# Hybrid attention block on one core: the next block's logits are taken before the second map is added, the stick-breaking scan zeroes masked weights itself, and input sums and accumulating transfers get places in the engine orders

## The chip, the cores and the metric

The kernel runs on one core of a Trainium2 chip. The core has five engines with an instruction queue each: TensorE (PE, matrix products), VectorE (DVE, elementwise work and scans), ScalarE (ACT, lookups and copies), GpSimd (POOL, elementwise work and the DMAs that accumulate) and SyncE (SP, the other DMAs). Each queue is worked off in order; semaphores order the engines against each other. The metric is the device time of one execution in microseconds, lower is better.

## The reference, cut to what matters

512 tokens of width 1024 get 16 meta tokens in front (528 positions), a layer norm, and one large input projection. Its columns feed two attention branches: eight differential heads (two softmax maps each, the second subtracted with a learned factor `lam`) and sixteen stick-breaking heads. Both are causal. Gates, two branch projections, a merge, an output projection and a last layer norm follow.

```python
def diff_attn_block(q, k, v, q_pos, slopes, lam):
    ...
    s = jnp.where(dist >= 0, s + alibi[None, :, None], -jnp.inf)
    p = jax.nn.softmax(s, axis=-1)
    a = p[:, :, 0] - lam * p[:, :, 1]
    return jnp.einsum('bhqk,bhkd->bhqd', a.astype(v.dtype), v)

def stick_breaking_block(q, k, v, q_pos):
    k_pos = jnp.arange(k.shape[2])
    before = k_pos[None, :] < q_pos[:, None]
    z = jnp.einsum('bhqd,bhkd->bhqk', q, k).astype(jnp.float32) * (SB_HEAD_DIM ** -0.5)
    log_keep = jnp.where(before, jax.nn.log_sigmoid(-z), 0.0)
    suffix = lax.cumsum(log_keep, axis=3, reverse=True) - log_keep
    a = jnp.where(before, jnp.exp(jax.nn.log_sigmoid(z) + suffix), 0.0)
    return jnp.einsum('bhqk,bhkd->bhqd', a.astype(v.dtype), v)
```

## The kernel before

All tensors are float32. A product is made from a high part rounded to the PE's short float32 (`wh`, `hTh`) and a remainder (`wl`, `hTl`), in three matmuls: high by high, high by low, low by high. The weights come from HBM in halves of 128 x 512. For each half SP loads `raw` (L134), ACT casts it to `wh` (`hi`, L160) and DVE subtracts to get `wl` (`lo`, L165). `prep` does this four halves ahead of the half that PE multiplies, and then calls `fetch`, which issues loads as far as the ring buffers have room.

From the fourth unit on, keys and values of a unit are made together from seven products instead of eight (a Strassen-like scheme, `stage_kv`, matmuls at L626). It needs sums of the input, `tS` and `tl`, made once by `input_sums` (four calls; each has one small copy on POOL at L597, four DVE sums at L599 to L602, a cast on ACT at L604 and a subtraction on DVE at L605). It also needs sums of weight halves. For two of them, SP loads one half into a buffer `rawk` (L134) and a DMA issued by POOL adds the other half from HBM to it (L136, `accum_op`); DVE adds further ones (`add`, L147). The branch projections at the end do the same with `rawa`.

The middle of the program is a list of 16 units: eight differential heads (`d`), then eight pairs of stick-breaking heads (`s`). While PE makes the projections of the next units, `run` inserts the steps of the current unit at written times. For a `d` unit these are `d_scores`: for each of the four blocks of 128 queries (longest first: 528, 400, 272, 144 keys) and each of the two maps, PE makes logits (L692), DVE adds the bias and takes the row minimum (L775), ACT takes the exponential with its sum (L779). Then DVE takes reciprocals (L783), POOL scales the first map (L784) and multiplies the second factor by `nlam` (L785), and DVE adds the scaled second map into `apad` (L786). `transposed` turns `apad` on PE (L698, L703), ACT and DVE split it (`ah` L708, `al` L709), `d_values` multiplies by the values, and `d_norm` (with a Ln at L821 and an Exp at L823 on ACT) finishes the head one unit later. For an `s` unit, `s_scores` has ACT take two sigmoids per logit tile (L840, L842), POOL zero the weights on and right of the diagonal (L846), DVE run a product scan from the right (L848, against a mask `after` that holds the product at 1 over masked columns) and multiply (L849).

The order of the instructions on each engine is decided by the framework's scheduler, which lists instructions by a simulated timeline while it respects data dependencies. Two places are fixed by hand: `keep_order` holds the program order for the start and the tail, and `behind` chains chosen ACT instructions. `follow` adds such an order-only dependency between two instructions. In the middle part all else may be moved by the scheduler, also far ahead of where it was written.

Of the kernel before, what the change touches and what calls it, by code (L numbers as in the profile page):

```python
# [44 lines left out]
def hybrid_block_kernel(ctx: ExitStack, tc: tile.TileContext, x, meta, emb_g, emb_b, w_in, b_gate,  # L45
# [70 lines left out]
    raws, split, sums, later = {}, [], {}, []  # L116
# [8 lines left out]
    def fetch(most=99):  # L125

        while state["l"] < len(loads) and most:
            l = state["l"]
            src, more, tag = loads[l]
            bufs, log = rings[tag]  # L130
            if len(log) >= bufs and left[log[-bufs]] or tag not in pools:
                return
            raw = pools[tag].tile([P, 4, P], F32, tag=tag, name=tag, bufs=bufs)
            nc.sync.dma_start(raw if l < WOUT else raw.rearrange("p a b -> p (a b)"), src)  # L134
            if more is not None:
                g.dma_start(raw, more, accum_op=ALU.add)  # L136
            raws[l] = raw
            log.append(l)
            state["l"] += 1
            most -= 1  # L140

    def add(h):

        first, second = items[h]
        one = sums.pop(True) if first is None else raws[first]
        raw = one if first is None else pools["sum"].tile([P, 4, P], F32, tag="sum", name="sum", bufs=1)
        v.tensor_tensor(raw, one, raws[second], op=ALU.add)  # L147
        for l in items[h]:
            if l is not None:
                left[l] -= 1  # L150
        sums[h] = sums[True] = raw

    def hi(h):

        assert len(split) == h
        item = items[h]
        raw = raw0[:, h // 2, ts(h % 2, 4)] if item is None else sums.pop(h) if isinstance(item, tuple) else raws[item]
        wh, wl = [wpool.tile([P, 4, P], F32R, tag=w, name=w, bufs=6) for w in ("wh", "wl")]
        split.append((raw, wh, wl))
        s.copy(wh, raw)  # L160
# [30 lines left out]
    def behind(name, on=True):  # L191

        if on:
            ins = nc.cur_bb.bb.instructions[-1]
            if name in state:
                follow(ins, state[name])
            state[name] = ins

    def keep_order(first, engines=ORDERED):

# [318 lines left out]
    with tc.tile_pool(name="att", bufs=1) as ap:  # L519
# [17 lines left out]
        after, staged = [], []  # L537


        K = [ap.tile([P, 2, L], F32R, name=f"k{c}") for c in range(2)]  # L540
# [209 lines left out]
        def d_scores(unit, h):  # L750

            A = unit["A"]


            bias = ap.tile([P, L], F32, tag="bias", name="bias", bufs=2)
            if h == 0:
                g.iota(bias, pattern=[[-1, L]], base=400, channel_multiplier=1, allow_small_or_imprecise_dtypes=True)
                g.affine_select(bias, bias, pattern=[[-1, L]], compare_op=ALU.is_ge, fill=1e30, base=400,
                                channel_multiplier=1)
            g.tensor_scalar(bias, biases[-1] if h else bias, 0.5 if h else -0.5, None, op0=ALU.mult)  # L760
            biases.append(bias)
            a = apads[h % 2]
            mn = ap.tile([P, NB, 2, 2], F32, tag="mn", name="mn", bufs=2)
            zs = ap.tile([P, NB, 2], F32, tag="zs", name="zs", bufs=2)
            rz = ap.tile([P, NB, 2], F32, tag="rz", name="rz", bufs=2)
            for i in reversed(range(NB)):
                nk = NKEY[i]
                e = [E[c][:, ZOFF[i]:ZOFF[i] + nk] for c in range(2)]
                for c in range(2):
                    m = mn[:, i, c, :]  # L770
                    for n, (ps, k0, use) in enumerate(logits(A[c], K[c], i)):
                        if n == 1:
                            yield
                        b0 = 384 - P * i + k0
                        v.tensor_tensor_reduce(e[c][:, k0:k0 + use], ps[:, :use], bias[:, b0:b0 + use], -1.0, 3e38,  # L775
                                               ALU.add, ALU.min, m[:, n:n + 1])
                    if nk > 512:
                        v.tensor_tensor(m[:, 0:1], m[:, 0:1], m[:, 1:2], op=ALU.min)
                    s.activation(e[c], e[c], AF.Exp, scale=-1.0, bias=m[:, 0:1], accum_out=zs[:, i, c:c + 1])  # L779
                    if c == 0:  # L780
                        yield
                r = rz[:, i, :]
                v.reciprocal(r, zs[:, i, :])  # L783
                g.tensor_scalar(e[0], e[0], r[:, 0:1], None, op0=ALU.mult)  # L784
                g.tensor_tensor(r[:, 1:2], r[:, 1:2], nlam, op=ALU.mult)  # L785
                v.scalar_tensor_tensor(a[:, AOFF[i]:AOFF[i] + nk], e[1], r[:, 1:2], e[0], op0=ALU.mult, op1=ALU.add)  # L786
                yield

        def d_values(unit, ta):
            (vh, vl), vf = unit["V"]  # L790
# [39 lines left out]
        def s_scores(unit, c, first):  # L830
# [3 lines left out]
            for i in reversed(range(NB)):  # L834
# [7 lines left out]
                    s.activation(sg[:, o], ps[:, :use], AF.Sigmoid)  # L842
                    behind("act", first)

                own = sg[:, ds(z0 + nk - P, P)]
                g.affine_select(own, own, pattern=[[-1, P]], compare_op=ALU.is_gt, fill=0.0, base=0, channel_multiplier=1)  # L846
                rev = om[:, z0:z0 + nk][:, ::-1]
                v.tensor_tensor_scan(rev, rev, after[0][:, L - nk:][:, ::-1], 1.0, ALU.mult, ALU.max)  # L848
                v.tensor_tensor(a[:, ds(AOFF[i], nk - 1)], sg[:, ds(z0, nk - 1)], om[:, ds(z0 + 1, nk - 1)],  # L849
                                op=ALU.mult)  # L850
                yield
# [22 lines left out]
        def spread(gen, t0, dt, count):  # L874
            return [(t0 + dt * m, lambda: next(gen)) for m in range(count)]
# [12 lines left out]
        for u, (kind, n) in enumerate(UNITS):  # L888
# [9 lines left out]
            if u + 4 in (SEVEN + 1, SEVEN + 2):  # L898
                if not tS:
                    tS.append(ypool.tile([P, KT, L], F32R, tag="ys", name="tS"))  # L900
                for m in range(2):
                    steps.append((5.0 + 6.0 * m, lambda k=2 * (u + 3 - SEVEN) + m: input_sums(k)))
            if kind == "d":
                ta = {}
                steps += spread(d_scores(unit, n), 0.0, TD[0], 10)
                parts = transposed(ta, apads[n % 2], "d")
                steps += [(TD[1] + 0.7 * m, f) for m, f in enumerate(parts)]
                steps.append((TD[2], lambda: d_values(unit, ta)))
                pending = [(3.0 if n < 7 else 5.8, lambda unit=unit, n=n: d_norm(unit, n))]
# [268 lines left out]
```

## Time and profile before

| | value |
|---|---|
| time, median of 3 runs | 742.61 us (742.55 to 744.74) |
| the profiled execution | 746.39 us, of which the profile's span is 744.7 us |
| mean granted TensorE clock | 0.983 |
| PE busy | 716.7 us, 4546 matmuls |
| DVE busy | 597.4 us |
| ACT busy | 441.2 us |
| POOL busy | 212.3 us |
| HBM read and written | 82.53 MB and 7.86 MB |

The profile is of one execution. Times in its timeline are in microseconds from the start of the span. A row of the timeline gives start, duration, engine, line, operation, what is written and read, and in brackets the idle time of the engine just before it with the instruction that ended it. A row of the table by stretches gives, for each stretch of time, its length and the busy time of PE, of the PE's weight loads, of DVE, ACT and POOL with the number of instructions, the granted clock, and the DMA share and rate. PE, POOL and DVE overlap; the program ends when PE's products and the tail after them are done. SPq and POOLq mean the queue of an engine that issues DMAs.

### The profile page before, as it was taken

What the parts mean: (1) busy time and instruction counts of PE and PEld (TensorE: products, weight loads), DVE (VectorE), ACT (ScalarE), POOL (GpSimd) and SP (SyncE); (2) the same over time, 40 slices, a digit from 0 to 9 for tenths busy, and PEclk for the clock granted to TensorE, in tenths of its full rate; (3) what the DMA queues carried; (4) which work ended last, traced back from release to release, by engine and by line L of the source; (5) the groups of instructions that cost most, each with busy time, mean ns of one, the idle gap of its engine ahead of it and who ended that gap; (6) DMA issues with size and microseconds to landing.
All of it is one profiled execution on the core that took longest, in us unless ns stands there. A gap on an engine that the chain in (4) does not pass through costs nothing.

```text
span 744.7 us, 13453 instructions
## 1 busy us (share of the span) xinstructions
PE 716.7 (96%) x4546; PEld 651.2 (87%) x4546; DVE 597.4 (80%) x1214; ACT 441.2 (59%) x1043; POOL 212.3 (29%) x269
## 2 busy tenths in 40 slices
PE   8899999998999898999999999999999999999995
PEld 8799999987988787888989898988888998899885
DVE  6986678887888767979797989878566778688897
ACT  5675667676667966656656565656544555656300
POOL 3343453453463313232323121214002201240002
PEclk9989999999999998999999999999999999999998
DMA  9374444647555544455655524395229747787802
GB/s 291 89 153 119 133 98 114 162 104 164 141 113 130 136 128 108 135 123 144 140 158 117 140 90 126 104 304 147 71 83 184 157 100 180 147 169 186 320 27 105
DMA packets 160135, 105.02 MB, mean 141 GB/s; under 512 B 7441, under 2 KB 148146, under 8 KB 160066
## 3 DMA queue, kind: packets, MB, share of 16 engines
q1 hardware_dynamic: 137762, 91.04, 41.5%
q0 software_dynamic: 21984, 12.06, 12.8%
q10 hardware_dynamic: 320, 1.06, 0.4%
q8 instruction: 36, 0.59, 0.3%
q14 instruction: 33, 0.27, 0.1%
HBM read 82.53 MB, written 7.86 MB: 121 GB/s over the span
## 4 chain that ended last, share of the span: by engine, by line
PE 80%; DVE 7%; DMA 4%; POOL 3%; issue 3%; ACT 3%; SPq 0%; ACTq 0%; DVEq 0%; POOLq 0%
PE q L626 15%; PE ps L460 11%; PE ps L459 11%; PE ps L461 11%; PE q L985 9%; PE ps L475 6%; PE sc L692 5%; PE t L698 3%; DMA lgb<-in_ln_b_dram 1%; PE t L703 1%; DMA rawk<-in_w_in_dram 1%; PE bank L350 1%; PE av L862 1%; PE av L863 1%; POOL e L784 1%
## 5 line engine op out<-in xcount | busy, mean ns | idle before, releaser
L165 DVE TENSOR_TENSOR wl<-raw,wh 128x512 fp32r<-128x512 f32 x168 | 121.2, 726 | 41.7 <-ACT wh L160 40.2
L460 PE MATMUL ps<-hTl,wh 128*128 128x512 f32 x368 | 146.7, 399 | 0.0
L459 PE MATMUL ps<-hTh,wh 128*128 128x512 f32 x368 | 145.8, 396 | 0.0
L461 PE MATMUL ps<-hTh,wl 128*128 128x512 f32 x368 | 145.3, 395 | 0.0
L160 ACT CAST wh<-raw 128x512 fp32r<-128x512 f32 x168 | 102.9, 621 | 35.5 <-PE ps L460 20.6
L461 PEld LDWEIGHTS ps<-hTh,wl 128*128 128x128 f32 x368 | 69.6, 189 | 12.9
L459 PEld LDWEIGHTS ps<-hTh,wh 128*128 128x128 f32 x368 | 69.6, 189 | 12.8
L460 PEld LDWEIGHTS ps<-hTl,wh 128*128 128x128 f32 x368 | 69.6, 189 | 12.1
L692 PE MATMUL sc<-k,A 128*128 128x264 f32 (+3 forms) x320 | 66.7, 301 | 4.1 <-ACT e L842 2.3
L846 POOL TENSOR_SCALAR_AFFINE_SELECT e<-e 128x128 f32<-128x128 f32 x64 | 43.6, 702 | 93.0 <-ACT e L842 84.5
L985 PE MATMUL q<-gh,wl 128*128 128x256 f32 x224 | 63.9, 285 | 0.0
L985 PE MATMUL q<-gl,wh 128*128 128x256 f32 x224 | 63.7, 284 | 0.0
L985 PE MATMUL q<-gh,wh 128*128 128x256 f32 x224 | 63.2, 282 | 0.2 <-ACT t L994 0.2
L784 POOL TENSOR_SCALAR e<-e,rz 128x528 f32<-128x528 f32 (+3 forms) x32 | 46.1, 1441 | 56.9 <-DVE rz L783 56.9
L136 POOL DMA_DIRECT2D rawk<-in_w_in_dram x24 | 32.4, 1381 | 99.5 <-DMA rawk<-in_w_in_dram 62.2
L709 DVE TENSOR_TENSOR al<-t,ah 128x512 fp32r<-128x512 f32 (+2 forms) x88 | 45.7, 525 | 18.4 <-ACT ah L708 11.2
L692 PEld LDWEIGHTS sc<-k,A 128*128 128x128 f32 x320 | 51.4, 192 | 9.2 <-ACT e L842 2.7
L848 DVE TENSOR_TENSOR_SCAN e<-e,after 128x528 f32<-128x528 f32 (+1 forms) x64 | 55.4, 871 | 4.8 <-ACT e L840 4.6
L708 ACT CAST ah<-t 128x512 fp32r<-128x512 f32 (+2 forms) x88 | 40.1, 464 | 30.0 <-PE t L698 21.9
L626 PE MATMUL q<-tS,wh 128*128 128x264 f32 x192 | 56.0, 292 | 0.8 <-DVE A L552 0.7
L626 PE MATMUL q<-tl,wh 128*128 128x264 f32 x192 | 55.4, 289 | 0.0
L626 PE MATMUL q<-tS,wl 128*128 128x264 f32 x192 | 55.0, 288 | 0.0
(278 smaller groups left out, 1976.7 us busy)
## 6 DMA issues: line engine op xcount, KB each, us to landing
raw<-in_w_in_dram SPq DMA_DIRECT2D x140, 256.0 KB, 3.1
k<-ks SPq DMA_DIRECT2D x60, 132.0 KB, 2.7
rawk<-in_w_in_dram SPq DMA_DIRECT2D x24, 256.0 KB, 3.4
rawk<-in_w_in_dram POOLq DMA_DIRECT2D x24, 256.0 KB, 5.2
raw<-in_w_out_dram SPq DMA_DIRECT2D x16, 256.0 KB, 3.7
k<-ks SPq DMA_DIRECT2D x60, 66.0 KB, 2.2
raw<-in_w_br_diff_dram SPq DMA_DIRECT2D x12, 256.0 KB, 3.4
raw<-in_w_br_sb_dram SPq DMA_DIRECT2D x12, 256.0 KB, 4.2
```

What stands on the lines that cost most here:

```text
L160: s.copy(wh, raw)
L165: eng.tensor_tensor(wl, raw, wh.bitcast(F32), op=ALU.subtract)
L459: pe.matmul(ps, wh[:, k % 4, :], hTh[:, k, M:], start=(k == 0), stop=False)
L460: pe.matmul(ps, wh[:, k % 4, :], hTl[:, k, M:], start=False, stop=False)
L461: pe.matmul(ps, wl[:, k % 4, :], hTh[:, k, M:], start=False, stop=(k == KT - 1))
L475: pe.matmul(ps[:, :H2], a[:, k % 4, :], b[:, k, ts(c, H2)], start=(k == 0 and m == 0), stop=(k == KT - 1 and m == 2))
L626: pe.matmul(bank, a[:, k, :], b, start=start and k == 0 and j == 0, stop=k == 3 and j == 2, skip_group_check=not start)
L692: pe.matmul(ps[:, :n], q, K[:, m, k0:k0 + n], start=(m == 0), stop=(m == 1))
L709: v.tensor_tensor(l, t[:, o:o + w], h.bitcast(F32), op=ALU.subtract)
L784: g.tensor_scalar(e[0], e[0], r[:, 0:1], None, op0=ALU.mult)
L848: v.tensor_tensor_scan(rev, rev, after[0][:, L - nk:][:, ::-1], 1.0, ALU.mult, ALU.max)
L985: pe.matmul(bank, a[:, k, :], b[:, n, k, :], start=start and k == 0 and m == 0, stop=k == 3 and m == 2, skip_group_check=not start)
```

## The change

Four edits are made.

1. In `d_scores` the last step of a block (DVE adds the second map, formerly L786) is put off: it is kept in a list `last` and issued in the next block, once the first map's logits of that block have been taken. The last block's one gets an extra step, so `d_scores` has 11 steps instead of 10. On POOL the small product with `nlam` comes before the scaling of the first map.
2. In `s_scores` the zeroing of masked weights on POOL (L846) is removed. The scan starts at 0 and takes the larger of the product and a matrix `diag` that is 1 on the diagonal only, so that it is 0 right of the diagonal, 1 on it and the product left of it. `diag` is a zeroed tile with a copy of the identity.
3. `input_sums` is wrapped in `placed`, which makes the first instruction that it issues on each of PE, DVE, ACT and POOL follow the instruction written before it on that engine. The scheduler can't move it ahead of that place.
4. The accumulating transfers are no longer issued in `fetch`. They wait in `second` and are issued by `added`, two calls of `prep` later for `rawk` (or earlier, if `hi` or `add` wants the sum), and are `placed` on POOL. For `rawa` they are issued at once, as before, and placed.

```diff
             if more is not None:
-                g.dma_start(raw, more, accum_op=ALU.add)
+                second[l] = lambda raw=raw, more=more: g.dma_start(raw, more, accum_op=ALU.add)
+                later.append((state["n"] + (2 if tag == "rawk" else 0), lambda l=l: added(l)))
+                later.sort(key=lambda x: x[0])
+                if tag == "rawa":
+                    added(l)
...
+    def added(l):
+
+        if l in second:
+            placed(second.pop(l), ORDERED[3:])
+
     def add(h):
 
-        first, second = items[h]
+        first, other = items[h]
+        for l in items[h]:
+            added(l)
...
         item = items[h]
+        added(item)
...
+    def placed(work, engines=ORDERED):
+
+        ins = nc.cur_bb.bb.instructions
+        n = len(ins)
+        work()
+        for e in engines:
+            new = next((i for i in ins[n:] if i.engine == e), None)
+            old = next((ins[m] for m in range(n - 1, max(n - 400, 0), -1) if ins[m].engine == e), None)
+            if new is not None and old is not None:
+                follow(new, old)
...
+            last = []
             for i in reversed(range(NB)):
...
                     if c == 0:
                         yield
+                        if last:
+                            placed(last.pop(), ORDERED[1:2])
                 r = rz[:, i, :]
                 v.reciprocal(r, zs[:, i, :])
+                g.tensor_tensor(r[:, 1:2], r[:, 1:2], nlam, op=ALU.mult)
                 g.tensor_scalar(e[0], e[0], r[:, 0:1], None, op0=ALU.mult)
-                g.tensor_tensor(r[:, 1:2], r[:, 1:2], nlam, op=ALU.mult)
-                v.scalar_tensor_tensor(a[:, AOFF[i]:AOFF[i] + nk], e[1], r[:, 1:2], e[0], op0=ALU.mult, op1=ALU.add)
+                last.append(lambda i=i, e=e, r=r, nk=NKEY[i]: v.scalar_tensor_tensor(
+                    a[:, AOFF[i]:AOFF[i] + nk], e[1], r[:, 1:2], e[0], op0=ALU.mult, op1=ALU.add))
                 yield
+            placed(last.pop(), ORDERED[1:2])
+            yield
...
-                own = sg[:, ds(z0 + nk - P, P)]
-                g.affine_select(own, own, pattern=[[-1, P]], compare_op=ALU.is_gt, fill=0.0, base=0, channel_multiplier=1)
                 rev = om[:, z0:z0 + nk][:, ::-1]
-                v.tensor_tensor_scan(rev, rev, after[0][:, L - nk:][:, ::-1], 1.0, ALU.mult, ALU.max)
+                v.tensor_tensor_scan(rev, rev, diag[0][:, L - nk:][:, ::-1], 0.0, ALU.mult, ALU.max)
...
-                    steps.append((5.0 + 6.0 * m, lambda k=2 * (u + 3 - SEVEN) + m: input_sums(k)))
+                    steps.append((5.0 + 6.0 * m, lambda k=2 * (u + 3 - SEVEN) + m: placed(lambda: input_sums(k))))
...
-                steps += spread(d_scores(unit, n), 0.0, TD[0], 10)
+                steps += spread(d_scores(unit, n), 0.0, TD[0], 11)
...
-                    after.append(ap.tile([P, L], F32, tag="bias", name="after", bufs=2))
-                    g.memset(after[0], 0.0)
-                    own = after[0][:, L - P:]
-                    g.affine_select(own, own, pattern=[[-1, P]], compare_op=ALU.is_gt, fill=1.0, base=0, channel_multiplier=1)
+                    diag.append(ap.tile([P, L], F32, tag="bias", name="diag", bufs=2))
+                    g.memset(diag[0], 0.0)
+                    g.tensor_copy(diag[0][:, L - P:], ident)
```

The scheduler decides again on the whole middle part, so the orders differ in more places than the edits name. Three places follow. Line numbers of the changed kernel are higher: L177 stands for L165, L436 for L413, L591 for L568, L342 for L319, L799 for L775, L810 for L785, L811 for L784, L838 for L809, L783 for L760, L869 and L871 for L840 and L842, L850 and L852 for L821 and L823, L803 for L779, L172 for L160, L660 and L662 for L637 and L639.

The first is DVE at the start of the middle part, where the first keys `k` are split. Before (`hF` are the input sums, `nlam` the factor of the second map, `A` the queries):

```order
L319 SCALAR_TENSOR_TENSOR A_173<-bank,A_173 64x512
L165 TENSOR_TENSOR wl<-raw_87,wh 128x512
L599 TENSOR_TENSOR hF<-hF 128x264 x2
L165 TENSOR_TENSOR wl<-raw_87,wh 128x512
L413 TENSOR_SCALAR nlam<-lexp 128x1
L599 TENSOR_TENSOR hF<-hF 128x264 x2
L600 TENSOR_TENSOR hF<-hF 128x264 x3
L568 TENSOR_TENSOR k_455<-ps,k_455 64x264
L600 TENSOR_TENSOR hF<-hF 128x264
L601 TENSOR_TENSOR hF<-hF 128x264 x4
L602 TENSOR_TENSOR hF<-hF 128x264
L568 TENSOR_TENSOR k_456<-ps,k_456 64x264
```

And the same place of DVE now, with the first reduction of logits (L799) behind it:

```order
L342 SCALAR_TENSOR_TENSOR A_173<-bank,A_173 64x512
L177 TENSOR_TENSOR wl<-raw_87,wh 128x512 x2
L436 TENSOR_SCALAR nlam<-lexp 128x1
L591 TENSOR_TENSOR k_455<-ps,k_455 64x264
L591 TENSOR_TENSOR k_456<-ps,k_456 64x264
L342 SCALAR_TENSOR_TENSOR A_174<-bank,A_174 64x512
L342 SCALAR_TENSOR_TENSOR A_175<-bank,A_175 64x512
L591 TENSOR_TENSOR k_455<-ps,k_455 64x264
L591 TENSOR_TENSOR k_456<-ps,k_456 64x264
L799 ISA e_453,mn<-sc,bias 128x264
```

The sums of the input have left this place; the four subtractions for `k` and the queries stand directly behind `nlam`. The sums now stand in the units 1 to 3, between other work.

The second is POOL around the start of a differential unit with seven products (`e` is the first map, `rz` the reciprocals, `sql` a part of the norm, `rawk` a weight sum in the making). Before:

```order
L136 DMA rawk<-in_w_in_dram 128x4x128
L760 TENSOR_SCALAR bias<-bias 128x528
L784 TENSOR_SCALAR e_453<-e_453,rz 128x144
L785 TENSOR_TENSOR rz<-rz,nlam 128x1
L136 DMA rawk<-in_w_in_dram 128x4x128
L784 TENSOR_SCALAR e_453<-e_453,rz 128x528
L785 TENSOR_TENSOR rz<-rz,nlam 128x1
L136 DMA rawk<-in_w_in_dram 128x4x128
L784 TENSOR_SCALAR e_453<-e_453,rz 128x400
L785 TENSOR_TENSOR rz<-rz,nlam 128x1
```

And now, for the same kind of stretch:

```order
L783 TENSOR_SCALAR bias<-bias 128x528
L810 TENSOR_TENSOR rz<-rz,nlam 128x1
L811 TENSOR_SCALAR e_453<-e_453,rz 128x144
L136 DMA rawk<-in_w_in_dram 128x4x128 x2
L810 TENSOR_TENSOR rz<-rz,nlam 128x1
L811 TENSOR_SCALAR e_453<-e_453,rz 128x528
L810 TENSOR_TENSOR rz<-rz,nlam 128x1
L811 TENSOR_SCALAR e_453<-e_453,rz 128x400
L810 TENSOR_TENSOR rz<-rz,nlam 128x1
```

The two accumulating transfers of a unit now stand together behind the last block (144 keys) of a unit and ahead of the next unit's first block. Before, they stood at two places, one of them between the blocks of 528 and of 400 keys. In the stick-breaking units POOL had eight L846 a unit among them; now it has only the two gate products and the two transfers.

The third is ACT at the change from the differential to the stick-breaking units (a table load stands where the next lookup function is in another table; `r` is the norm, `e` with L840 a sigmoid). Before:

```order
L840 ACT_TABLE_LOAD
L840 ACTIVATE e_454<-sc 128x264
L842 ACTIVATE e_453<-sc 128x264
L779 ACT_TABLE_LOAD
L779 ACTIVATE e_454,zs<-e_454,mn 128x144
L160 CAST wh<-raw 128x512
L639 COPY kvt<-q 128x264
L821 ACT_TABLE_LOAD
L821 ACTIVATE r<-ms,epsr 128x512
L160 CAST wh<-raw 128x512
L641 COPY kvt<-q 128x264
L823 ACT_TABLE_LOAD
```

And now:

```order
L869 ACT_TABLE_LOAD
L869 ACTIVATE e_454<-sc 128x264
L871 ACTIVATE e_453<-sc 128x264
L850 ACT_TABLE_LOAD
L850 ACTIVATE r<-ms,epsr 128x512
L803 ACT_TABLE_LOAD
L803 ACTIVATE e_454,zs<-e_454,mn 128x144
L852 ACTIVATE r<-r 128x512
L172 CAST wh<-raw 128x512
L662 COPY kvt<-q 128x264
L172 CAST wh<-raw 128x512
L664 COPY kvt<-q 128x264
```

The exponential of the last block and that of the norm now stand in a row behind the logarithm's table, and one table load (L823) is gone; the two casts and the copy that stood among them come after.

More of the change, by code (lines that the diff above doesn't have):

```diff
@@ L115, in hybrid_block_kernel @@
     raw0 = ypool.tile([P, 4, KT, P], F32, tag="ys", name="raw0")
-    raws, split, sums, later = {}, [], {}, []
+    raws, second, split, sums, later = {}, {}, [], {}, []
     rings = {"raw": (6, []), "rawk": (4, []), "rawa": (4, [])}
@@ L140, in fetch @@
             most -= 1
+    def added(l):
+        if l in second:
+            placed(second.pop(l), ORDERED[3:])
     def add(h):
-        first, second = items[h]
+        first, other = items[h]
+        for l in items[h]:
+            added(l)
         one = sums.pop(True) if first is None else raws[first]
         raw = one if first is None else pools["sum"].tile([P, 4, P], F32, tag="sum", name="sum", bufs=1)
-        v.tensor_tensor(raw, one, raws[second], op=ALU.add)
+        v.tensor_tensor(raw, one, raws[other], op=ALU.add)
         for l in items[h]:
@@ L536, in hybrid_block_kernel @@
         E = [ap.tile([P, ZW], F32, name=f"e{c}") for c in range(2)]
-        after, staged = [], []
+        diag, staged = [], []
         K = [ap.tile([P, 2, L], F32R, name=f"k{c}") for c in range(2)]
```

## The prediction

> **What bounds the kernel now.** I read the page's shares first, then the chain that ended last, then PE's busy time stretch by stretch, and last the timeline where PE stood idle.
>
> ```profile
> span 744.7 us, 13453 instructions
> PE 716.7 (96%) x4546; PEld 651.2 (87%) x4546; DVE 597.4 (80%) x1214; ACT 441.2 (59%) x1043; POOL 212.3 (29%) x269
> ...
> PEclk9989999999999998999999999999999999999998
> ...
> PE 80%; DVE 7%; DMA 4%; POOL 3%; issue 3%; ACT 3%; SPq 0%; ACTq 0%; DVEq 0%; POOLq 0%
> ```
>
> PE is the bound: it is busy for 716.7 of 744.7 us, and 80% of the chain lies on it. The change removes no matmul. It can give only what PE loses: idle time, and time at a lower granted clock. So the question is where those losses are. In the next rows the columns are the stretch, its length, and the busy time of PE, PE loads, DVE, ACT and POOL, then clock and DMA.
>
> ```profile
> 32.80:37.20 4.40, 0.70 (x5) 0.37 (x3) 4.31 (x13) 2.17 (x5) 4.27 (x10) 0.92 0.81 234
> 37.20:44.20 7.00, 7.00 (x35) 7.00 (x36) 6.76 (x9) 5.74 (x10) 6.91 (x6) 0.57 1.20 147
> 70.00:117.00 47.00, 47.00 (x333) 44.43 (x333) 33.91 (x94) 31.05 (x84) 18.31 (x21) 1.00 0.43 109
> 117.00:141.00 24.00, 24.00 (x171) 22.65 (x170) 20.87 (x55) 18.65 (x49) 11.97 (x12) 1.00 0.51 116
> 141.00:165.00 24.00, 22.83 (x157) 20.93 (x156) 20.03 (x51) 16.21 (x43) 10.66 (x10) 1.00 0.57 133
> 159.00:166.00 7.00, 6.04 (x47) 5.59 (x46) 6.41 (x16) 4.48 (x13) 4.72 (x7) 1.00 0.61 135
> 165.00:190.00 25.00, 22.60 (x148) 21.10 (x147) 19.75 (x52) 17.08 (x45) 9.09 (x11) 0.93 0.62 142
> 190.00:250.00 60.00, 56.45 (x398) 52.67 (x398) 49.29 (x121) 44.92 (x107) 28.07 (x36) 1.00 0.61 138
> 250.00:260.00 10.00, 7.67 (x36) 6.25 (x35) 8.81 (x14) 8.92 (x21) 2.71 (x6) 0.83 0.34 104
> 283.60:293.60 10.00, 6.45 (x33) 6.10 (x32) 7.28 (x13) 5.11 (x14) 5.01 (x7) 0.66 0.49 105
> 330.00:545.00 215.00, 214.87 (x1312) 191.77 (x1311) 174.30 (x308) 129.08 (x327) 54.38 (x64) 1.00 0.49 136
> ```
>
> The losses are these. Start: 4.40 - 0.70 = 3.7 us idle, then 7.00 us at 0.57, which is 3.0 us of clock: 6.7. Differential units, 141 to 250: idle 1.17 + 2.40 + 3.55 = 7.1, clock 22.60 x 0.07 = 1.6: 8.7. Change of branch, 250 to 260: idle 2.33, clock 7.67 x 0.17 = 1.3; 283.6 to 293.6: idle 3.55, clock 6.45 x 0.34 = 2.2; together 9.4. From 330 to 545, where nearly all of the stick-breaking work lies, PE misses 0.13 us. So 24.8 us can be won at most, and all of it before 294 us.
>
> **Start (edit 3).** These rows show why PE stood.
>
> ```profile
> 22.45 0.85 POOL L597 COPY hF<-hM 128x32 f32<-128x32 f32 x4 [5.29 <-DVE hM L391]
> ...
> 31.59 0.37 ACT L567 CAST k<-ps 64x264 fp32r<-64x264 f32 x1 [3.63 <-DVE nlam L413]
> ...
> 35.70 0.43 DVE L568 TENSOR_TENSOR k<-ps,k 64x264 fp32r<-64x264 f32 x1
> 35.75 1.07 ACT L604 CAST tS<-hF 128x1056 fp32r<-128x1056 f32 x1 [1.33 <-POOL bias L757]
> ...
> 34.12 0.48 PE L692 MATMUL sc<-k,A 128*128 128x264 f32 x2 [1.16 <-POOL k L542]
> 37.15 0.59 PE L475 MATMUL ps<-hTh,wh 128*128 128x264 f32 x1 [2.55 <-ACT k L569]
> L599 DVE TENSOR_TENSOR hF<-hF 128x264 f32<-128x264 f32 x4 | 1.5, 428 | 0.0
> L605 DVE TENSOR_TENSOR tl<-hF,tS x4: 1240/1254/1495, 37.2 to 43.6; 128x1056 fp32r<-128x1056 f32 x4
> ```
>
> (The last two rows are groups: count, busy us and mean ns; and min, median and max ns.) PE waited for the casts of `k`, and those waited for DVE and ACT, which were making input sums. In the new order `nlam` stands behind two L165 without the pair of sums (2 x 0.43 us at most, some 0.7), so the first cast starts near 30.9. Four casts of 0.37 and two subtractions of 0.43 that only wait for each other end at about 33.2 instead of 37.1. POOL's zeroing of `k`, which PE's first logits wait for (34.12), also starts 0.7 us earlier. PE's gap of 3.7 us shrinks to some 0.7 us. A stretch with 0.96 us idle (159 to 166) keeps the clock at 1.00, so the 3.0 us of clock go too. I take **-6.0**; ends -3.0 (the clock drops anyway) and -6.7.
>
> The work is not gone. Sixteen sums of 0.43 us and four subtractions of 1.25 us, 11.8 us of DVE, now lie in units 1 to 3; the four casts (1.07) fit on ACT, busy 31.05 of 47 there, and the four copies (0.85 in all) on POOL, busy 18.31. DVE has 33.91 us in 70 to 117 and would have 45.7 of 47. In 117 to 141 it carries 20.87 of 24 (87%) while PE is never idle, so up to 0.87 x 47 = 40.9 us is covered by what a row shows, and 4.8 us is not. Some of the last sums fall into the third unit, whose products need `tl`; there DVE is at 87% already. I take **+4.0**; ends 0 (all is packed beside PE) and +11.8 (none is).
>
> **Differential units (edits 1 and 4).** One of the stalls, in order:
>
> ```profile
> 159.22 1.64 DVE L786 SCALAR_TENSOR_TENSOR apad<-e,rz,e 128x400 f32<-128x400 f32 x1 [1.26 <-POOL rz L785]
> ...
> 178.56 1.28 POOL L136 DMA_DIRECT2D rawk<-in_w_in_dram  x1 [5.45 <-DMA rawk<-in_w_in_dram]
> 179.35 2.14 POOL L784 TENSOR_SCALAR e<-e,rz 128x528 f32<-128x528 f32 x1
> 181.69 0.77 DVE L786 SCALAR_TENSOR_TENSOR apad<-e,rz,e 128x528 f32<-128x528 f32 x1 [2.43 <-POOL rz L785]
> 184.10 0.64 DVE L786 SCALAR_TENSOR_TENSOR apad<-e,rz,e 128x400 f32<-128x400 f32 x1 [0.34 <-POOL rz L785]
> 185.97 0.39 PE L626 MATMUL q<-hTh,wh 128*128 128x264 f32 x1 [2.40 <-DVE vT L646]
> ```
>
> POOL sat 5.45 us in the accumulating DMA's wait, its scaling came late, DVE waited 2.43 us in L786 with `vT` queued behind, and PE waited 2.40 us for `vT`. Both links are cut: the transfer stands behind the last block, and L786 stands one block later. What is late next is the transfer itself, behind the last block's scaling:
>
> ```profile
> 193.66 1.52 POOL L784 TENSOR_SCALAR e<-e,rz 128x144 f32<-128x144 f32 x1 [0.23 <-DVE rz L783]
> 245.64 0.65 POOL L784 TENSOR_SCALAR e<-e,rz 128x144 f32<-128x144 f32 x1 [0.96 <-DVE rz L783]
> 197.87 0.62 ACT L160 CAST wh<-rawk 128x512 fp32r<-128x512 f32 x1
> DMA to landing us min/median/max: 4.4/5.3/9.4
> ```
>
> Now the transfer would be issued at about 193.7 + 0.6 (an undisturbed L784 of 144 keys takes 0.65, at 245.64) and land 5.3 us later at 199.6, while ACT comes to the cast at 197.87: 1.7 us of waiting, on ACT, with the exponentials and `ah` queued behind it and DVE waiting for both. Six pairs stand so. SP still issues the first loads in `fetch`, and the buffers come free as before, so its queue does not move. Weights are prepared four halves ahead, so PE does not wait for that cast itself; I let it see 0.7 of the 1.7 us. Of 8.7 us, 6 x 0.7 = 4.2 come back: **-4.5**; ends 0 and -8.7.
>
> **Change of branch (edits 2 and 4).**
>
> ```profile
> 284.03 1.29 POOL L136 DMA_DIRECT2D rawk<-in_w_in_dram  x1 [5.48 <-ACT e L840]
> 284.82 1.63 POOL L846 TENSOR_SCALAR_AFFINE_SELECT e<-e 128x128 f32<-128x128 f32 x3
> 285.68 0.64 DVE L849 TENSOR_TENSOR apad<-e,e 128x399 f32<-128x399 f32 x1 [3.19 <-POOL e L846]
> 287.29 0.50 PE L863 MATMUL av<-al,V 128*128 128x160 f32 x1 [3.55 <-DVE al L709]
> ...
> 251.69 1.28 ACT L840 ACT_TABLE_LOAD   x1
> 253.71 0.52 PE L692 MATMUL sc<-k,A 128*128 128x272 f32 x2 [2.33 <-ACT e L842]
> ```
>
> At 284 POOL hangs in the transfer, the zeroing comes late, DVE waits for it with `al` behind, and PE waits 3.55 us. Without the zeroing DVE never waits for POOL here: 3.55 + 2.2 = 5.7 go. At 251 ACT changes tables; the new order has one load of 1.28 us less, which leaves 2.33 - 1.28 = 1.05 us of gap, about the size that kept its clock at 159: 1.3 + 1.3 = 2.6 go. **-8.3**; ends -3.6 (only the idle part of the first) and -9.4. Everywhere else the 64 zeroings lie beside a PE that is full (0.13 us idle in 215), so edit 2 gives nothing there; the scan keeps its shapes.
>
> The Trainium skill (TensorE: Matmul & The Clock Gate, Part 1) says the clock falls after an idle window of about 3.4 us. The trace disagrees: 2.33 us were followed by 0.83 over 250 to 260. By the page that 1.3 us would have another cause and stay, and the sum would be 1.3 us smaller.
>
> **Sum.** -6.0 + 4.0 - 4.5 - 8.3 = -14.8 us, against the profiled execution of 746.39 us (span 744.7) 731.6. That execution is 3.8 us above the median of 742.61; the difference taken from the median gives **727.8, so 728**.
>
> **Rivals.** *DVE full in units 1 to 3*: all 11.8 us are seen by PE: -14.8 + 7.8 = -7.0, 736. For it speaks 45.7 of 47 us; against it that PE was never idle at 87%. A longer L786 would bring it nearer: put off, it can meet POOL's scaling of the next block, and 1.64 us at 159.22 against 0.64 at 184.10 shows how much. The Trainium skill (SBUF — State Buffer, Who interferes with whom) says that a DVE instruction with two SBUF inputs contends with a GpSimd instruction that reads SBUF. L786 has two; the 1.64 us agree, and by the page this case would be the likelier one.
>
> *Sums late as well*: the differential units give nothing either: -7.0 + 4.5 = -2.5, 740.
>
> *Slower*: the accumulating transfers land late. If PE sees each of the six waits whole, the differential gain is gone (-10.3 left) and 12.5 us, 2.1 a pair, make the kernel slower by 0.3% (2.2 us). That is a landing of 5.7 us instead of 5.3, within the row's 9.4. At 2.4 us each: +4.1, 747. Against it: those halves are wanted four products later.
>
> *Better*: DVE packs everything and every listed loss goes: -24.8, 718.
>
> That an edit doesn't do what it says is excluded by the orders; whether the scheduler's new places suit is in the cases.
>
> **How the numbers follow.** Forecast (723 to 735) 0.52, DVE full 0.16, sums late as well 0.10, slower 0.10, better 0.12. The range takes in the forecast and the two smaller gains and leaves out the slower case and most of the better one: 720 to 741. About 0.3%, 2.2 us, is what a measurement can tell from no change. The case at 740 lies on that border and counts 0.07 as same and 0.03 as faster: faster 0.83, same 0.07, slower 0.10.
>
> **What would show it.** Start: PE's products of L475 resume before 34.5 us, clock 1.00 after. Units 1 to 3: DVE above 90%, PE idle up to 4 us, ended by `tl` or `vT`. Differential units: no wait of DVE for `rz`; ACT waits of 1 to 2 us for `rawk`. Change of branch: `al` no longer ends a PE wait, one gap of about 1 us ended by a sigmoid. It is wrong if PE waits for weights, or if the clock drops at gaps of 1 us.

## The result, and the profile after

| | before | after |
|---|---|---|
| median of 4 runs each | 743.67 us | 756.38 us |
| lowest to highest | 742.55 to 746.83 us | 754.60 to 756.91 us |
| profiled execution (span) | 746.39 us (744.7) | 756.91 us (755.1) |

The ratio is 1.016 with a 95% interval of 1.012 to 1.020: the changed kernel is **slower**, where 728 us had been forecast. Ratios, here and below, are of fast runs alone: of all the kernels only f_at_once had slow ones, two of ten, and without them its median is 748.45 us. The page of after, its engines and its chain that ended last:

```profile
span 755.1 us, 13319 instructions
PE 718.7 (95%) x4546; PEld 648.6 (86%) x4546; DVE 588.1 (78%) x1214; ACT 438.0 (58%) x1042; POOL 172.6 (23%) x205
...
PE 57%; DVE 12%; DMA 11%; issue 10%; POOL 5%; ACT 3%; SPq 0%; POOLq 0%; DVEq 0%; ACTq 0%
```

DVE and POOL have less to do than before, as the edits meant, yet PE's part of the chain fell from 80% to 57% and that of DMA rose from 4% to 11%. The groups by line say which DMA. First POOL's transfers before, then after (count, busy us, mean ns, idle time ahead of the group and what ended it; last, the page's list of DMA issues, with us from issue to landing, before and after):

```profile
L136 POOL DMA_DIRECT2D rawk<-in_w_in_dram x24 | 32.4, 1381 | 99.5 <-DMA rawk<-in_w_in_dram 62.2 <-DVE sg L489 7.0 <-DVE v4d L674 6.6
rawk<-in_w_in_dram POOLq DMA_DIRECT2D x24, 256.0 KB, 5.2
```

```profile
L136 POOL DMA_DIRECT2D rawk<-in_w_in_dram x24 | 31.8, 1567 | 0.4 <-issue 0.4
L172 ACT CAST wh<-rawk 128x512 fp32r<-128x512 f32 x24 | 14.8, 617 | 13.5 <-DMA rawk<-in_w_in_dram 8.3 <-PE ps L483 3.8 <-PE q L649 1.4
L158 DVE TENSOR_TENSOR sum<-rawk,raw 128x512 f32<-128x512 f32 x12 | 8.3, 691 | 19.4 <-DMA rawk<-in_w_in_dram 17.1 <-issue 2.3
rawk<-in_w_in_dram POOLq DMA_DIRECT2D x24, 256.0 KB, 7.0
```

Before, POOL waited 62.2 us for the first loads so that it could issue the accumulating transfers, and nobody waited for these. Now POOL waits for nothing there, and DVE (17.1 us) and ACT (8.3 us) wait for the transfers. The 2.3 us that the row of L158 puts down to issue are one more such wait: it ends at 149.62, and the third pair has landed at 149.54. So 11 of the twelve pairs are waited for, 27.7 us in all. One of the twelve pairs in the timeline of after:

```profile
111.60 0.64 POOL L811 TENSOR_SCALAR e<-e,rz 128x144 f32<-128x144 f32 x1
112.19 2.64 POOL L136 DMA_DIRECT2D rawk<-in_w_in_dram  x2
...
121.52 0.69 DVE L158 TENSOR_TENSOR sum<-rawk,raw 128x512 f32<-128x512 f32 x1 [2.44 <-DMA rawk<-in_w_in_dram]
122.13 0.58 DVE L732 TENSOR_TENSOR al<-t,ah 128x416 fp32r<-128x416 f32 x1
122.63 0.15 DVE L802 TENSOR_TENSOR mn<-mn 128x1 f32<-128x1 f32 x1
122.70 1.25 DVE L628 TENSOR_TENSOR tl<-hF,tS 128x1056 fp32r<-128x1056 f32 x1
...
124.00 0.39 PE L649 MATMUL q<-tl,wh 128*128 128x264 f32 x1 [3.58 <-DVE tl L628]
```

The pair is issued behind the scaling of the unit's last block, at 112.19. DVE wants it at 119.1, sits 2.44 us in L158 until it has landed, and `al`, `mn` and `tl` stand behind. PE then waits 3.58 us, and the wait carries the name of `tl`: the one that is named last is not the one that was late first.

Where the time went is read from a mark that every kernel has, the first transposition `tv` of the values of each unit on PE (L659, now L682). The table gives how far a kernel is behind (+) or ahead (-) of the kernel before at that mark, in us of the profiled executions. The columns right of after are experiments below. Each column is one execution, and the times of one kernel spread over 2 to 8 us, so a microsecond in it says little.

| mark (before, us) | after | edit 4 alone | 1+2+3 | 3 alone | 2+3 | tie in s units only |
|---|---|---|---|---|---|---|
| unit 0 (47.40) | -5.89 | +0.45 | -6.06 | -6.00 | -6.34 | -6.22 |
| unit 3 (123.26) | +4.83 | +1.14 | +3.46 | +2.13 | +1.89 | +6.19 |
| unit 4 (148.53) | +4.33 | +1.69 | -1.49 | -4.20 | -4.45 | +0.68 |
| unit 8 (261.95) | +9.26 | +6.47 | -4.69 | -7.80 | -7.89 | -7.11 |
| unit 9 (301.24) | +5.08 | +11.19 | -8.35 | -6.38 | -11.18 | -11.90 |
| unit 15 (507.84) | +8.58 | +12.10 | -8.04 | -6.34 | -11.07 | -5.72 |
| PE's last (736.34) | +10.36 | +16.00 | -8.07 | -3.57 | -11.04 | -5.19 |

The start gains what was forecast. All of it and more is gone by unit 3, and after the change of branch (units 8 to 9) 3.5 us more go in the stick-breaking part, where the forecast had nothing. A mark that is late is not yet time lost, since PE takes products of later units in between (3 alone: +2.13 at unit 3, -4.20 at unit 4).

### The profile page after: what moved, and what is told of

It reads as the page before. It is cut to its first block, busy times and chain, and to the rows that moved or that the text cites. A ratio compares the mean times of both kernels' runs of the same rounds, so it can differ in the third digit from the quotient of the medians.

```text
span 755.1 us, 13319 instructions
## 1 busy us (share of the span) xinstructions
PE 718.7 (95%) x4546; PEld 648.6 (86%) x4546; DVE 588.1 (78%) x1214; ACT 438.0 (58%) x1042; POOL 172.6 (23%) x205
## 4 chain that ended last, share of the span: by engine, by line
PE 57%; DVE 12%; DMA 11%; issue 10%; POOL 5%; ACT 3%; SPq 0%; POOLq 0%; DVEq 0%; ACTq 0%
PE q L1011 9%; PE ps L482 8%; PE ps L483 8%; PE ps L484 8%; DMA rawk<-in_w_in_dram 7%; PE q L649 7%; PE ps L498 4%; PE sc L715 3%; DVE wl L177 2%; DMA raw<-in_w_out_dram 2%; PE t L721 2%; POOL e L811 1%; DMA k<-ks 1%; PE bank L373 1%; POOL rawk L136 1%
## 5 line engine op out<-in xcount | busy, mean ns | idle before, releaser
L483 PE MATMUL ps<-hTl,wh 128*128 128x512 f32 x368 | 145.1, 394 | 0.0
L177 DVE TENSOR_TENSOR wl<-raw,wh 128x512 fp32r<-128x512 f32 x168 | 117.0, 702 | 35.4 <-ACT wh L172 34.1
L172 ACT CAST wh<-raw 128x512 fp32r<-128x512 f32 x168 | 102.9, 621 | 39.5 <-PE ps L483 25.8
L875 DVE TENSOR_TENSOR_SCAN e<-e,diag 128x528 f32<-128x528 f32 (+1 forms) x64 | 56.2, 879 | 4.6 <-ACT e L869 4.3
L731 ACT CAST ah<-t 128x288 fp32r<-128x288 f32 (+3 forms) x88 | 39.7, 466 | 26.9 <-DVE al L732 14.5
L803 ACT ACTIVATE e<-e,mn 128x528 f32<-128x528 f32 (+3 forms) x64 | 36.7, 574 | 19.0 <-DVE mn L799 10.0
L649 PE MATMUL q<-hTh,wh 128*128 128x264 f32 x144 | 43.5, 302 | 4.3 <-DVE vT L669 4.3
L1011 PEld LDWEIGHTS q<-gh,wh 128*128 128x128 f32 x224 | 42.6, 190 | 2.1 <-ACT t L1016 1.0
```

The lines of the kernel that those rows point to most:

```text
L177: eng.tensor_tensor(wl, raw, wh.bitcast(F32), op=ALU.subtract)
L483: pe.matmul(ps, wh[:, k % 4, :], hTl[:, k, M:], start=False, stop=False)
L649: pe.matmul(bank, a[:, k, :], b, start=start and k == 0 and j == 0, stop=k == 3 and j == 2, skip_group_check=not start)
L731: s.copy(h, t[:, o:o + w])
L875: v.tensor_tensor_scan(rev, rev, diag[0][:, L - nk:][:, ::-1], 0.0, ALU.mult, ALU.max)
L1011: pe.matmul(bank, a[:, k, :], b[:, n, k, :], start=start and k == 0 and m == 0, stop=k == 3 and m == 2, skip_group_check=not start)
```

## The experiments

Theory 1 was that the transfers land late, theory 2 that the moved input sums fill DVE, theory 3 that any new order costs. All ratios are against the kernel before on the same chip. Its median there was 743.67 us for after, 745.45 for the four kernels that follow, 745.73 for the two f kernels, e13 and e23, and 746.41 for the three g kernels and e234; where medians of different groups are compared, the ratio is the safer figure.

| run | edits | median us | ratio, 95% interval |
|---|---|---|---|
| after | 1 2 3 4 | 756.38 | 1.016 (1.012 to 1.020) |
| e123_transfers_back | 1 2 3 | 740.71 | 0.9945 (0.9925 to 0.9964) |
| e4_transfers_only | 4 | 766.00 | 1.0281 (1.0243 to 1.0320) |
| e124_sums_back | 1 2 4 | 757.12 | 1.0172 (1.0138 to 1.0206) |
| e3_sums_only | 3 | 742.30 | 0.9954 (0.9933 to 0.9975) |
| f_at_once | 1 2 3, 4 without the delay | 749.33 | 1.0027 (0.9997 to 1.0057) |
| f_late_free | 1 2 3, 4 without the tie | 740.97 | 0.9951 (0.9929 to 0.9972) |
| g_tie_s | 1 2 3, 4 tied in s units only | 741.38 | 0.9942 (0.9903 to 0.9981) |
| e13_scan_back | 1 3 | 745.07 | 0.9987 (0.9971 to 1.0003) |
| e23_add_back | 2 3 | 735.04 | 0.9870 (0.9836 to 0.9903) |
| g_add_free | 1 untied, 2 3 | 744.72 | 0.9977 (0.9957 to 0.9997) |
| g_swap | 2 3, POOL's half of 1 | 736.76 | 0.9875 (0.9857 to 0.9892) |
| e234_add_back | 2 3 4 | 752.69 | 1.0087 (1.0061 to 1.0114) |

**Transfers or sums.** Four kernels, with edit 4 or edit 3 taken out or alone.

```diff
-                second[l] = lambda raw=raw, more=more: g.dma_start(raw, more, accum_op=ALU.add)
-                later.append((state["n"] + (2 if tag == "rawk" else 0), lambda l=l: added(l)))
...
+                g.dma_start(raw, more, accum_op=ALU.add)
```

> The changed kernel with edit 4 alone undone: the accumulating transfers are issued in fetch again and the scheduler places them. Theory 1 (the transfers land late and DVE and ACT wait for them): the waits for rawk and the gaps behind them go, 8 to 12 us of the 756: 744 to 748. Theory 2 (the moved input sums make units 1 to 3 late, 12 us there): those units still lose 10 to 12 us and the time is 752 to 757. Theory 3 (what costs is that the scheduler orders the middle part anew, whatever the edit): no definite sign, any time between 738 and 757, with the losses at other places than in the changed kernel.

> The kernel before with edit 4 alone: accumulating transfers two preps later and tied to their place on POOL. Theory 1: 8 to 12 us slower than before, 752 to 756, with DVE's add and ACT's cast waiting for rawk. Theory 2: within 2 us of before, 742 to 746. Theory 3: a difference from before that isn't the opposite of what undoing edit 4 in the changed kernel gives.

For the other two, `placed(lambda: input_sums(k))` becomes `input_sums(k)` in the changed kernel, and the reverse in the kernel before.

> The changed kernel with edit 3 alone undone: the input sums go where the scheduler wants them, as before. Theory 2: the start loses its 5.9 us again, units 1 to 3 lose their 12 us no more: 749 to 751. Theory 1: the start loses 5.9 us and units 1 to 3 still wait for rawk, of their 12 us at most the 4 go that the prediction gave to the sums: 757 to 762. Theory 3: neither.

> The kernel before with edit 3 alone: input sums tied to their places. Theory 2: start 6 us earlier, units 1 to 3 12 us longer: 749 to 751. Theory 1: start 6 us earlier, units 1 to 3 some 4 us longer, as the prediction had it: 741 to 743. Theory 3: neither.

Undoing edit 4 gives back 15.7 us, more than theory 1 asked for, and edit 4 alone costs 2.8%: more than all four edits together. Edit 3 alone is 0.5% faster than before (theory 1: 741 to 743; measured 742.3), so theory 2 falls. Theory 3 falls as the main cause: edit 4 costs 2.8% alone, and undoing it among the others gives 2.1% back. With edit 3 out and edit 4 in, 757.12 is at theory 1's lower end: there the sums' place is worth nothing that shows. Groups of edits 1 to 3 (its L168, L154 are L172, L158) with the transfers as before:

```profile
L136 POOL DMA_DIRECT2D rawk<-in_w_in_dram x24 | 32.8, 1388 | 123.4 <-DMA rawk<-in_w_in_dram 43.1 <-DVE wl L173 16.7 <-DMA k<-ks 9.5
L168 ACT CAST wh<-rawk 128x512 fp32r<-128x512 f32 x24 | 14.8, 618 | 9.8 <-PE ps L479 7.7 <-issue 1.1 <-PE q L645 0.7
L154 DVE TENSOR_TENSOR sum<-rawk,raw 128x512 f32<-128x512 f32 x12 | 8.2, 685 | 0.3 <-DMA raw<-in_w_in_dram 0.2
```

POOL waits again (43.1 us), and the 25.4 us of waiting for `rawk` on DVE and ACT are gone.

**Which half of edit 4.** It has a delay (two preps) and a tie (behind the POOL instruction written ahead of it). One kernel drops each:

```diff
-                later.append((state["n"] + (2 if tag == "rawk" else 0), lambda l=l: added(l)))
+                later.append((state["n"], lambda l=l: added(l)))
...
-            placed(second.pop(l), ORDERED[3:])
+            second.pop(l)()
```

> The changed kernel with the delay of edit 4 taken out: the accumulating transfers are issued in the same call of prep as their first loads, still tied to the POOL instruction written ahead of them. Theory 1a (tied to POOL's attention work, which runs some six preps behind the weight preparation, the transfer is issued about 9 us ahead of its use and needs 7; two preps, some 6 us, more lead end the waits for rawk): waits of DVE and ACT for rawk fall from 25 us to under 6, 742 to 748. Theory 1b (the tie itself costs, since the 2.6 us in which a pair is issued then stand among POOL's attention work wherever they are put): 751 to 757, with DVE waiting for rz or e instead of rawk.

> The changed kernel with the tie of edit 4 taken out: the accumulating transfers are still written two preps later, but the scheduler may move them on POOL. Theory 1a: the scheduler issues each some 4 us after its first load has been issued, 10 to 25 us ahead of its use; no waits of DVE or ACT for rawk, 739 to 744. Rival (the delay is what costs, wherever POOL then takes them): 750 to 757, with the waits for rawk still there.

Without the tie all of the loss is gone (740.97 against 740.71 with edit 4 out), though the transfers are still written two preps later. Without the delay half of it goes, with runs from 741.40 to 754.79, but not in the way that theory 1a had it. The groups of f_at_once:

```profile
L172 ACT CAST wh<-rawk 128x512 fp32r<-128x512 f32 x24 | 14.8, 618 | 16.8 <-DMA rawk<-in_w_in_dram 7.3 <-PE ps L483 5.3 <-PE q L649 4.1
L158 DVE TENSOR_TENSOR sum<-rawk,raw 128x512 f32<-128x512 f32 x12 | 8.3, 688 | 17.9 <-DMA rawk<-in_w_in_dram 17.0 <-DVE wl L177 0.9
```

The waits are 24.3 us as against 25.4: not under 6. They moved. In its timeline only one of them (1.11 us) is left ahead of 250 us, and the others stand at the change of branch and in the stick-breaking units. So there were two places to tell apart:

```diff
-            placed(second.pop(l), ORDERED[3:])
+            if l >= 60:
+                placed(second.pop(l), ORDERED[3:])
+            else:
+                second.pop(l)()
```

> The changed kernel with the tie of the accumulating transfers kept only from the stick-breaking units on (and for rawa, as in the changed kernel); those of the differential units are written two preps later but free. Theory 1c (the tie costs in both parts: in the differential units because POOL's scaling runs behind the weight preparation, in the stick-breaking ones because POOL's gate products wait for DVE): the trace of the changed kernel loses 3.5 us between the units 9 and 15 and 1.6 us behind them, so 740.8 + 5 = 745 to 747. Rival (only the tie to the scaling of the differential units costs; what was lost later followed from it): 739 to 742.

The time, 741.4, is what the rival said; the marks say theory 1c. From unit 9 to unit 15 this kernel goes from -11.90 to -5.72, a loss of 6.2 us where edits 1 to 3 lose 0.3. By unit 9 its profiled execution is 3.6 us ahead of that of edits 1 to 3, for no reason that was tried, and that hid it. Its four runs spread over 7.7 us, so the total alone could not have told the two apart. One of the waits in the timeline (L517 is the gate product, L161 the sum, L755 a part of the values):

```profile
273.52 0.37 SPq L134 DMA_DIRECT2D rawk<-in_w_in_dram  x1
...
332.45 1.29 POOL L517 TENSOR_TENSOR ys<-sg,ys 128x512 f32<-128x512 f32 x1 [11.75 <-DVE ys L897]
333.68 2.62 POOL L136 DMA_DIRECT2D rawk<-in_w_in_dram  x2
...
343.49 0.69 DVE L161 TENSOR_TENSOR sum<-rawk,raw 128x512 f32<-128x512 f32 x1 [5.02 <-DMA rawk<-in_w_in_dram]
...
345.77 0.28 PE L889 MATMUL av<-a,v4s 128*128 128x32 f32 x1 [2.89 <-DVE a L755]
```

The later of the two first loads of this pair, the ninth, had been issued by SP at 273.52, so the data lay ready for more than 50 us. The ninth pair in edits 1 to 3, where it is free, and the sum that uses it:

```profile
269.31 1.35 POOL L136 DMA_DIRECT2D rawk<-in_w_in_dram  x1 [4.21 <-DMA rawk<-in_w_in_dram]
280.16 1.28 POOL L136 DMA_DIRECT2D rawk<-in_w_in_dram  x1 [9.50 <-DMA k<-ks]
...
330.42 0.69 DVE L154 TENSOR_TENSOR sum<-rawk,raw 128x512 f32<-128x512 f32 x1 [0.23 <-DMA raw<-in_w_in_dram]
```

Tied, the pair sits behind a gate product that waits 11.75 us for DVE, and goes 5 us ahead of the time at which DVE wants it (343.49 - 5.02 = 338.47). Free, it goes 50 us ahead. Stretches from unit 9 to unit 15 of edits 1 to 3, after and g_tie_s:

```profile
292.90:499.80 206.90, 206.39 (x1281) 184.63 (x1280) 173.90 (x312) 129.78 (x328) 25.11 (x18) 1.00 0.54 147
```

```profile
306.30:516.40 210.10, 207.42 (x1279) 183.83 (x1278) 174.28 (x311) 128.02 (x325) 30.25 (x22) 1.00 0.57 148
```

```profile
289.30:502.10 212.80, 208.16 (x1279) 185.43 (x1277) 174.29 (x313) 128.74 (x328) 31.16 (x22) 0.99 0.56 145
```

PE is idle for 0.51 us, 2.68 us and 4.64 us. The rest of the difference in length is PE's busy time, 1.03 and 1.77 us longer than in edits 1 to 3; its cause was not looked for.

**Edit 2.** The zeroing on POOL is put back, the transfers are as before.

```diff
+                own = sg[:, ds(z0 + nk - P, P)]
+                g.affine_select(own, own, pattern=[[-1, P]], compare_op=ALU.is_gt, fill=0.0, base=0, channel_multiplier=1)
...
-                v.tensor_tensor_scan(rev, rev, diag[0][:, L - nk:][:, ::-1], 0.0, ALU.mult, ALU.max)
+                v.tensor_tensor_scan(rev, rev, diag[0][:, L - nk:][:, ::-1], 1.0, ALU.mult, ALU.max)
```

> Edits 1 and 3 alone: transfers as before, the zeroing on POOL in the stick-breaking units back (edit 2 undone too). If edit 2 is what takes 3.6 us from the change of branch, as the prediction had it, this is 3.6 us or more above edits 1 to 3 together (740.7): 744 to 747. If the gain there comes from elsewhere, it is within 2 us of them.

It is 4.4 us above edits 1 to 3 by the medians, where 3.6 or more was expected, and 3.1 by the ratios. The marks agree: from unit 8 to unit 9 edit 4 alone, which has the zeroing, loses 4.7 us, and after gains 4.2. The wait for `al` is back at the place where the prediction had seen it. PE's rows of this kernel, then PE's only wait at that place in after:

```profile
287.24 0.34 PE L888 MATMUL av<-al,V 128*128 128x160 f32 x1 [2.44 <-DVE al L728]
...
293.06 0.33 PE L722 MATMUL t<-idents,apad 128*128 128x128 f32 x1 [1.00 <-DVE al L728]
```

```profile
293.17 0.28 PE L886 MATMUL av<-a,v4s 128*128 128x32 f32 x1 [0.50 <-DVE a L752]
```

**Edit 1.** The second map is added at the end of its own block again, with transfers as before and as in after; then edit 1 untied, and its half on POOL alone.

```diff
+                v.scalar_tensor_tensor(a[:, AOFF[i]:AOFF[i] + nk], e[1], r[:, 1:2], e[0], op0=ALU.mult, op1=ALU.add)
-                last.append(lambda i=i, e=e, r=r, nk=NKEY[i]: v.scalar_tensor_tensor(
-                    a[:, AOFF[i]:AOFF[i] + nk], e[1], r[:, 1:2], e[0], op0=ALU.mult, op1=ALU.add))
```

> Edits 2 and 3 alone: transfers as before, the second map added at the end of its own block again (edit 1 undone too). If putting off L812 takes the waits for rz out of the differential units (4.5 us in the prediction), this is 3 to 6 us above edits 1 to 3 together: 744 to 747. If those waits come from the transfers on POOL and not from the place of L812, it is within 2 us of 740.7.

> The changed kernel with edit 1 alone undone. If the costs of edit 1 (5.7 us with transfers as before) and of the tied transfers add up: 756.4 - 5.7, 749 to 752. If they hide behind each other (the late transfers already bound the units): 755 to 758. If edit 1 helps the tied transfers, as the prediction had it for the waits for rz: 759 to 763.

> Edits 1 to 3, transfers as before, with the second map's addition still written one block later but no longer tied on DVE. Theory 2a (the tie of L812 on DVE is what makes edit 1 cost 5.7 us): 734 to 737, as without edit 1. Theory 2b (the cost is in the other half of edit 1, the swap on POOL, or in putting the addition off as such): 739 to 742.

> Edits 2 and 3 with the half of edit 1 that concerns POOL alone: the product with nlam comes before the scaling of the first map, the addition stays in its own block. If the swap costs: 739 to 742. If it is the putting off that costs: 734 to 737, as edits 2 and 3 without the swap (735.0).

Neither expectation of the first run came true: without edit 1 the kernel is 5.7 us faster, 735.0, the fastest of this study and 1.3% faster than before. With the transfers of after it is 3.7 us by the medians and 5.4 by the ratios, so the two costs about add up. The tie is not what costs (untied: 744.7, rather worse), nor the swap on POOL (736.8): putting the addition off is. The largest block's addition in edits 2 and 3, and in edits 1 to 3:

```profile
L805 DVE SCALAR_TENSOR_TENSOR apad<-e,rz,e 128x528 f32<-128x528 f32 x8 | 6.7, 837 | 8.1 <-POOL rz L804 8.1
```

```profile
L808 DVE SCALAR_TENSOR_TENSOR apad<-e,rz,e 128x528 f32<-128x528 f32 x8 | 6.6, 820 | 0.4 <-POOL apad L940 0.2 <-POOL e L807 0.2
```

It does what it says, DVE's wait of 8.1 us is gone, and it gains nothing. What can be seen of its cost lies in units 1 to 3. Stretches from unit 0 to unit 3, in the order edits 2 and 3, edits 1 to 3, after:

```profile
41.10:125.10 84.00, 83.06 (x583) 77.76 (x581) 73.27 (x197) 57.86 (x150) 38.72 (x42) 1.00 0.52 129
```

```profile
41.30:126.70 85.40, 80.47 (x558) 75.25 (x557) 72.15 (x200) 57.53 (x150) 42.13 (x45) 0.97 0.49 122
```

```profile
41.50:128.10 86.60, 79.56 (x553) 74.54 (x552) 66.73 (x180) 55.44 (x143) 34.12 (x39) 0.98 0.49 118
```

PE is idle 0.94 us without edit 1, 4.93 us with it, 7.04 us with the tied transfers as well, and its granted clock is 1.00, 0.97 and 0.98. By unit 4 the first two are 2.96 us apart, and at PE's last product 2.97. The two executions differ by 4.2 us and the medians by 5.7, so a part of the cost was not located. That the added block stands between DVE's work for `tl` and `mn` and so delays it was read from the trace but not tried alone.

## Why the prediction was wrong, point by point

- **Start, -6.0: right.** It is -5.89 in after and -6.00 to -6.34 in the other kernels with edit 3 that the table of marks shows. PE never stops at 34 us, and the clock stays. After:

```profile
32.80:37.20 4.40, 4.25 (x35) 4.04 (x34) 1.93 (x4) 2.63 (x6) 4.09 (x6) 1.00 0.70 199
37.20:44.20 7.00, 7.00 (x60) 7.00 (x60) 5.80 (x16) 5.36 (x13) 1.05 (x1) 1.00 0.47 132
```

- **Units 1 to 3, +4.0: too high for the sums alone, far too low for after.** From unit 0 to unit 4, edit 3 alone gives back 1.8 us, edits 1 to 3 give back 4.6, after 10.2. The sums cost less than half of what was forecast, within its range; what was left out is that the first two pairs of transfers (81.86 and 112.19 in after) and the put-off additions fall into the same stretch.
- **Differential units, -4.5: the step that failed.** "Weights are prepared four halves ahead, so PE does not wait for that cast itself; I let it see 0.7 of the 1.7 us." The use that was measured was ACT's cast at 197.87, the fifth pair's. DVE's sum of that pair comes 4.4 us earlier, before the scaling behind which the transfer was to go has even started (193.66). Before, then the same pair in after:

```profile
193.48 0.67 DVE L147 TENSOR_TENSOR sum<-rawk,raw 128x512 f32<-128x512 f32 x1
```

```profile
197.81 1.09 POOL L811 TENSOR_SCALAR e<-e,rz 128x144 f32<-128x144 f32 x1
198.84 2.65 POOL L136 DMA_DIRECT2D rawk<-in_w_in_dram  x2
...
207.92 0.69 DVE L158 TENSOR_TENSOR sum<-rawk,raw 128x512 f32<-128x512 f32 x1 [2.57 <-DMA rawk<-in_w_in_dram]
```

  PE does not wait for the cast, but for what stands behind the waiting sum on DVE: 1.70 us for `al` at 92.69 and 3.58 us for `tl` at 124.00, right behind sums that waited 3.06 and 2.44 us. Its waits for `vT` (1.39 us at 218.6, 2.93 us at 245.1) were not followed back. The wait for a pair was forecast at 1.7 us and is 2.5 (27.7 / 11), and 11 pairs are waited for, not 6: of the twelve tied pairs six stand behind a scaling, one at the change of branch and five behind a gate product that had itself waited 6.1 to 15.3 us for DVE. From unit 4 to unit 8 after loses 4.9 us, where edits 1 to 3 gain 3.2. Edit 3 alone, with nothing of this term in it, gains 3.6, so not even that gain is the term's. Its other half, edit 1, removed its wait and cost 3.7 to 5.7 us instead of gaining.
- **Change of branch, -8.3: half right.** Edit 2 took the stall of `al` away: -4.18 from unit 8 to unit 9 in after, and 4.4 us in its own test (3.1 by the ratios). The other half did not come in after: one table load of ACT is gone there as forecast, but PE waits 2.93 us at 245.1 and 1.65 us at 258.6, with a clock of 0.89 over 240 to 272. In edits 1 to 3 the gap ended by a sigmoid is 0.89 us (1.05 forecast), and the clock holds:

```profile
251.55 0.52 PE L711 MATMUL sc<-k,A 128*128 128x272 f32 x2 [0.89 <-ACT e L867]
250.00:260.00 10.00, 8.94 (x50) 7.33 (x49) 9.09 (x18) 8.46 (x21) 0.20 (x2) 1.00 0.43 126
```

  That is luck as far as the prediction goes: this kernel has as many table loads as before (eight), so the reason that was given is not what shortened the gap. Nor do free transfers do it by themselves. In f_late_free, which has them too, the gap is 2.33 us and the clock 0.83 again (its profiled execution, 744.91 us, is among the slowest of its ten). What sets this gap stays open.

- **Stick-breaking part, 0: wrong for edit 4, right for edit 2.** Edits 1 to 3 are level with before there (-8.35 to -8.04). The forecast asked what edit 2 does in these units and did not ask where edit 4 puts the transfers once POOL has little else than gate products.
- **The rival "Slower" was the right one.** It had 747 at 2.4 us a pair, for six pairs and with the gains of the start and the branch kept; 756.38 was measured. Its landing of 5.7 us as the turning point was passed: the median is 7.0. (The row with 4.4/5.3/9.4 that it leaned on holds `rawa` as well; of the `rawk` transfers before, the slowest took 6.2 us.) It was given 0.10, with the halves "wanted four products later" against it: the place behind POOL's last scaling was measured against ACT's need and not against DVE's.

## What to carry to other kernels

An order-only tie to an engine makes a transfer wait for everything that the engine waits for: ask what the instruction ahead of it depends on, and how far the consumer of the transfer runs ahead of that. An engine that idles 62 us for a load may be the cheap place for a wait; moving the wait to the engine that uses the data moved it onto the path. Read a stall from the first late instruction of its queue, and an edit's worth from marks along the program, since two parts of a schedule can cancel in the total.

## What had not been expected of the hardware

Two accumulating transfers issued one behind the other land in 7.0 us in the median, where those that were mostly issued singly took 5.2. It is the second of a pair that is late: the first ones take 5.6 us in the median, the second ones 7.5. The Trainium skill (DMA: Bandwidth & Descriptors, "Anatomy of one DMA — SWDGE (gpsimd) path") fits the time of one transfer issued by GpSimd as 2.0 us and its bytes over 436e3 per us, which gives an estimate of 2.6 us for 256 KB. No accumulating transfer here is near it (the shortest before took 4.4 us). By that estimate the pair issued from 112.19 on would have landed by 117.4, ahead of its use at 119.1; it landed at 121.5, and the measurement decides.
